# The down projection of a gated FFN as one stage of seven block products by tokens, on one Trainium2 core

## The chip, the cores and the metric

The kernel runs on one core of a Trainium2 chip. The metric is the device time of one execution in microseconds (us). A core has TensorE (PE; its weight loads are shown apart as PEld), VectorE (DVE), ScalarE (ACT), GpSimd (POOL) and SyncE (SP, which here only issues DMAs); each works through its own list of instructions in order and waits on semaphores.

## The reference

One encoder block on 512 tokens of width 1024, in float32. Three token mixers are merged and projected; then comes the part that matters here, a feed-forward layer of width 2816, and a final norm:

```python
def conv_glu_ffn(h, w_up, w_conv, b_conv, w_down):
    a, u = jnp.split(h @ w_up, 2, axis=-1)
    return (jax.nn.gelu(dwconv3(a, w_conv, b_conv)) * u) @ w_down

x = x + merged @ w_out[l]
x = x + conv_glu_ffn(rms_norm(x, ffn_norm_g[l]), w_ffn_up[l], w_ffn_conv[l], b_ffn_conv[l], w_ffn_down[l])
return rms_norm(x, final_norm_g)
```

## The kernel before, in words

Activations lie with features on the 128 partitions and the 512 tokens along the free dimension: a tile is 128 features x 512 tokens. Every float32 product is made of three matmuls (`mm3`, lines 212 to 215): each operand is split into a rounded high part and the rest. For weights, ACT copies the raw tile to the high part (L195) and DVE subtracts (L196); high and low tiles have four slots each (`hi`, `lo`). For activations `split_act` does the same (L219, L220). SP loads the raw weights (L159) into three buffers, three blocks ahead. Scratch of 128x512 (`scr`, seven buffers) and large `unit` tiles (fifteen of 2112 columns) come from pools; PSUM has two pools of four banks (`mmps`, `atps`).

`x2` holds the residual stream after the mixers, features by tokens, eight tiles. The FFN runs in two halves of eleven feature tiles (`for hh in range(2)`). For each feature tile f, two up projections (`ua`, `uu`: 24 matmuls each) are followed by a chain: DVE scales and convolves (`conv`: L458, ACT L460, L461, L462), ACT and DVE make the gelu (L1414 to L1417), POOL multiplies by the norm factor `rb2` (L1418), DVE multiplies by the second projection (L1421), and the result U is split (L219, L220). After each half comes its down projection: eight output tiles of 11 x 3 matmuls, added to `x2` by DVE (L1428). In the second half the last tiles are handled by `last_tiles`: tiles 5, 6 and 7 for the first 256 tokens, tile 5 for the rest, then, for the last two blocks of 128 tokens, the last two tiles by tokens, with the norm's sums, the scaling and the stores in between. The squares for the final norm are summed over features (`acc3`); the stores go to three outputs, two of them by features, that the host puts together.

A scheduler places the instructions: it sets the order on each engine before the run, from the program's dependences and its own estimates; the source's order is a priority, not a promise.

Of the kernel before, what the change touches and what calls it, by code (L numbers as in the profile page):

```python
# [11 lines left out]
F32 = mybir.dt.float32  # L12
# [14 lines left out]
LF = KT - 2  # L27
# [35 lines left out]
def block_list():  # L63
# [39 lines left out]
BCOLS = {n: (lambda k: P) for n in ("mlk", "o", "xaq", "memk", "naq", "nak", "g", "out", "ua", "uu", "dn")}  # L103
# [3 lines left out]
BCOLS["dnl"] = lambda k: 256  # L107
# [3 lines left out]
def hybrid_block(ctx, tc, xg, xT, memT, wflat, vecs, gbias, nabias, outa, outb, outc):  # L111
# [55 lines left out]
    lw = []  # L167

    def lastw(k, m):

        if not lw:
            lw.extend(unit(F32R) for _ in range(4))
        q = slice(k % 8 * 256, k % 8 * 256 + m)
        return lw[k // 8][:, HI256:][:, q], lw[2 + k // 8][:, q]

    def emit_split(i):
# [47 lines left out]
    gbf = cp.tile([P, 272], F32, name="gbf")  # L224
    gb, gfin = gbf[:, :16], gbf[:, 16:]
# [224 lines left out]
    SY.dma_start(gbf, gbias.partition_broadcast(P))  # L450
# [803 lines left out]
    acc3 = cp.tile([P, S], F32, name="acc_3", tag="acc", bufs=1)  # L1254
    x2v = [u[:, :4 * S].rearrange("p (f s) -> p f s", f=4) for u in x2u]

    Hf = S // 2
    half = {}

    def power(v):  # L1260
        col = tiny(v.shape[-1])
        G.tensor_tensor(col, v, nhalf[:, :v.shape[-1]], op=ALU.pow)
        return col

    def last_tiles(U, UL_):

        ws = [w for i in range(3) for w in weights(("dnl", i))]
        w5 = weights(("dn", 1, LF - 1, 0)) + weights(("dn", 1, LF - 1, 1))  # L1270

        def half_tile(f, cs, at={}):
            ps = mmps()[:, :Hf]
            fs = slice((f - LF) * P, (f - LF + 1) * P) if f >= LF else slice(0, P)
            for k in range(HF):
                w = ws[k] if f >= LF else w5[k]
                mm3(ps, w[0][:, fs], w[1][:, fs], U[k][:, cs], UL_[k][:, cs], k == 0, k == HF - 1)
                if k in at:
                    at[k]()
            xf = x2[f][:, cs]  # L1280
            V.tensor_tensor(xf, ps, xf, op=ALU.add)
            sq = scr(Hf)
            A.activation(sq, xf, AF.Square)
            V.scalar_tensor_tensor(acc3[:, cs], acc3[:, cs], EPS * D / P if f == KT - 1 else 0.0, sq, op0=ALU.add, op1=ALU.add)
            A.activation(xf, xf, AF.Copy, scale=vcol("fin_g", f))

        for f in range(LF - 1, KT):
            half_tile(f, slice(0, Hf))

        parts = two_parts(acc3[:, :Hf], Hf)  # L1290

        def sum_a(i):
            if i == 0:
                half["s"] = atps()
            PE.matmul(half["s"][:, :Hf], onesr, parts[i], start=i == 0, stop=i == 1)
            if i == 1:
                half["r"] = rstd_wide(half["s"], Hf, None)

        def scale_a(eng, *tiles):
            for i in tiles:  # L1300
                eng.tensor_tensor(x2[i][:, :Hf], x2[i][:, :Hf], half["r"], op=ALU.mult)

        def store_a(i):
            SY.dma_start(outa[i * P:(i + 4) * P, :].rearrange("(f p) s -> p f s", p=P), x2v[i // 4][:, :, :Hf])

        half_tile(LF - 1, slice(Hf, S), {5: lambda: sum_a(0), 7: lambda: sum_a(1)})
        def out_a(i):
            scale_a(V, *range(i, i + 4))
            store_a(i)

        out_a(0)
        def row_b():

            pb = atps()
            PE.matmul(pb[:, :P], ones, half["e"], start=True, stop=True)
            o, tsl = half["o"], slice(2 * P, 3 * P)
            for u, n in ((0, 4), (1, LF - 4)):
                V.tensor_tensor(o[:, u * S:u * S + n * P].rearrange("p (f s) -> p f s", f=n), x2v[u][:, :n, tsl],
                                pb[:, :P].unsqueeze(1).to_broadcast([P, n, P]), op=ALU.mult)
            SY.dma_start(outc[:, :LF * P], o[:, :LF * P])  # L1320

        banks = [mmps(), mmps()]
        for t in range(2, NT):
            tsl = slice(t * P, (t + 1) * P)
            last = t == NT - 1
            bank = banks[t - 2]
            ps = bank[:, :256]
            pts = [atps() if last else None, mmps()]
            r = scr(256)

            def turn(i):
                PE.transpose(pts[i // 4][:, i % 4 * P:(i % 4 + 1) * P], x2[i][:, tsl], ident)

            def sums(sl):
                pc = atps()
                PE.matmul(pc[:, :1], acc3[:, sl], ones[:, 0:1], start=True, stop=True)
                v0 = tiny(1)
                V.tensor_scalar(v0, pc[:, :1], 1.0 / D, EPS, op0=ALU.mult, op1=ALU.add)
                return v0

            for k in range(HF):
                mm3(ps, U[k][:, tsl], UL_[k][:, tsl], ws[k][0], ws[k][1], k == 0, k == HF - 1)
                if k == 1 and last:

                    for i in range(LF, KT):
                        PE.matmul(ps[:, (i - LF) * P:(i - LF + 1) * P], x2[i][:, tsl], ident, start=False, stop=False)
                elif k == 1:
                    for i in range(LF, KT):
                        turn(i)
                    A.activation(r, pts[1][:, 256:], AF.Copy)  # L1350
                if not last and k == 4:
                    v0 = sums(tsl)

                    v1 = sums(slice(S - P, S))
                    V.scalar_tensor_tensor(banks[1][:, 256:257], v1, D ** 0.5, power(v1), op0=ALU.mult, op1=ALU.mult)
                    out_a(4)
                if last and k == 7:
                    row_b()
            if last:
                for i in range(LF):  # L1360
                    turn(i)
            sq, v = scr(257), tiny(1)
            if last:
                oa, ob = scr(), scr()

                A.activation(sq, bank[:, :257], AF.Square, scale=D ** -0.5, accum_out=v)
                A.activation(oa[:, 256:], pts[0][:, 256:], AF.Copy)
                col = power(v)
                A.activation(oa[:, :256], pts[0][:, :256], AF.Copy, scale=col)
                first = V.tensor_scalar(oa[:, 256:], oa[:, 256:], col, None, op0=ALU.mult).ins  # L1370
                SY.dma_start(outb[:, :512], oa)

                with tc.issue_after(first):
                    V.scalar_tensor_tensor(ob[:, 256:], ps, col, gfin, op0=ALU.mult, op1=ALU.mult)
                A.activation(ob[:, :256], pts[1][:, :256], AF.Copy, scale=col)
                A.dma_start(outb[:, 512:], ob)
                continue
            V.tensor_tensor(r, ps, r, op=ALU.add)
            ss = tiny(1)
            A.activation(sq[:, :256], r, AF.Square, accum_out=ss)  # L1380
            V.tensor_scalar(v, ss, 1.0 / D, v0, op0=ALU.mult, op1=ALU.add)
            col = power(v)
            half["e"] = scr(P)
            V.tensor_scalar(half["e"], ident, col, None, op0=ALU.mult)
            half["o"] = o = unit()
            V.scalar_tensor_tensor(o[:, LF * P:D], r, col, gfin, op0=ALU.mult, op1=ALU.mult)
            SY.dma_start(outc[:, LF * P:], o[:, LF * P:D])

    for hh in range(2):
        gu = [unit(F32R) for _ in range(6)]  # L1390
        UH = [gu[k // 4][:, (k % 4) * S:(k % 4 + 1) * S] for k in range(HF)]
# [162 lines left out]
```

## Time and profile before

| | |
|---|---|
| time, median of 3 runs | 873.49 us (873.18 to 873.82) |
| profiled execution, span from first to last instruction | 871.2 us; the rest of its time is not on the page, the median lies 2.3 us above the span |
| busy | PE 865.8, PEld 733.9, DVE 594.7, ACT 467.8, POOL 125.4 us |
| granted TensorE clock | 1.000 |
| DMA | 99.81 MB, mean 115 GB/s |

Rows of the profile: a group's row has line, engine, operation, what it writes and reads with shapes, count, busy time, mean duration in ns, then the idle time of the engine just before these instructions and what ended most of it. A row of the timeline has start, duration, engine, line and operation, and in brackets the wait before it. Matmul rows overlap: their pitch is the distance of starts.

### The profile page before, as it was taken

Reading aid. Unit: us, or ns where it says so; the run is one execution under the profiler, and the core shown is the slowest. Engines: PE = TensorE matmul, PEld = TensorE weight load, DVE = VectorE, ACT = ScalarE, POOL = GpSimd, SP = SyncE. Lnnn points to the kernel's source line nnn. Section 1 sums busy time; section 2 is a strip of 40 time slices with the busy share of each in tenths; the row PEclk is TensorE's granted clock in tenths of the full one; section 3 lists DMA queues with packets and bytes.
Section 4 is the critical chain, followed back from the end, with each engine's and each line's share of the span. In section 5 each row is a group of like instructions: output and inputs, shape, how many; then the busy total and the mean of one; then the engine's idle time right before and its main releaser. Section 6 shows DMA issues by size and latency. Waiting matters only on the chain.

```text
span 871.2 us, 12230 instructions
## 1 busy us (share of the span) xinstructions
PE 865.8 (99%) x4287; PEld 733.9 (84%) x4287; DVE 594.7 (68%) x1292; ACT 467.8 (54%) x981; POOL 125.4 (14%) x202
## 2 busy tenths in 40 slices
PE   9999999999999999999999999999999999999997
PEld 7898889888888888888888888888888888888887
DVE  7794698997477768897676558776633466666534
ACT  7563577764355658897534455444422344444532
POOL 0101100000344370600000002111100011111010
PEclk9999999999999999999999999999999999999999
DMA  8324643533343453533223433323233323232412
GB/s 281 101 75 147 196 140 89 169 107 115 93 132 82 113 146 112 160 116 122 99 96 109 144 109 97 98 96 98 78 98 113 102 96 97 96 98 87 141 35 97
DMA packets 39421, 99.81 MB, mean 115 GB/s; under 512 B 5688, under 2 KB 13880, under 8 KB 39360
## 3 DMA queue, kind: packets, MB, share of 16 engines
q1 hardware_dynamic: 31568, 92.32, 32.6%
q0 software_dynamic: 7360, 6.32, 3.4%
q8 instruction: 34, 0.56, 0.3%
q10 hardware_dynamic: 432, 0.39, 0.1%
q14 instruction: 27, 0.22, 0.1%
HBM read 94.80 MB, written 4.21 MB: 114 GB/s over the span
## 4 chain that ended last, share of the span: by engine, by line
PE 98%; DVE 1%; issue 0%; ACT 0%; POOL 0%; POOLq 0%
PE mm L213 29%; PE mm L215 29%; PE mm L214 29%; PE at L214 2%; PE at L213 2%; PE at L215 2%; PE at L982 1%; PE at L963 1%; PE at L944 0%; PE at L945 0%; PE at L765 0%; PE at L813 0%; PE at L1070 0%; PE at L243 0%; PE mm L422 0%
## 5 line engine op out<-in xcount | busy, mean ns | idle before, releaser
L213 PE MATMUL mm<-u,wh 128*128 128x512 f32 (+1 forms) x1072 | 414.3, 386 | 0.0
L215 PE MATMUL mm<-u,wl 128*128 128x512 f32 (+1 forms) x1072 | 411.8, 384 | 0.0
L214 PE MATMUL mm<-u,wh 128*128 128x512 f32 (+1 forms) x1072 | 411.5, 384 | 0.0
L195 ACT ACTIVATE wh<-wr 128x512 fp32r<-128x512 f32 (+2 forms) x298 | 184.2, 621 | 219.9 <-PE mm L214 177.2
L196 DVE TENSOR_TENSOR wl<-wr,wh 128x512 fp32r<-128x512 f32 (+3 forms) x300 | 203.4, 681 | 88.5 <-ACT wh L195 86.4
L215 PEld LDWEIGHTS mm<-u,wl 128*128 128x128 f32 x1072 | 201.3, 188 | 40.3 <-DVE wl L196 0.4
L213 PEld LDWEIGHTS mm<-u,wh 128*128 128x128 f32 x1072 | 201.5, 188 | 39.0 <-ACT wh L195 0.4
L214 PEld LDWEIGHTS mm<-u,wh 128*128 128x128 f32 x1072 | 201.5, 188 | 38.5
L1418 POOL TENSOR_TENSOR s<-s,rb 128x512 f32<-128x512 f32 x22 | 38.2, 1736 | 401.7 <-DVE s L1417 238.9
L540 POOL DMA_DIRECT2D u<-nav_d x128 | 62.5, 535 | 70.5 <-DVE X L220 24.3
L219 ACT ACTIVATE u<-s 128x512 fp32r<-128x512 f32 x26 | 16.4, 632 | 56.4 <-DVE s L1421 56.3
L1421 DVE TENSOR_TENSOR s<-mm,s 128x512 f32<-128x512 f32 x22 | 15.2, 690 | 23.9 <-POOL s L1418 23.9
L460 ACT ACTIVATE s<-pad,vec 128x512 f32<-128x512 f32 x30 | 24.4, 813 | 9.7 <-DVE pad L458 9.7
L220 DVE SCALAR_TENSOR_TENSOR u<-s,u 128x512 fp32r<-128x512 f32 x26 | 19.1, 733 | 14.8 <-ACT u L219 14.5
L461 DVE SCALAR_TENSOR_TENSOR s<-pad,vec,s 128x512 f32<-128x512 f32 x30 | 22.5, 750 | 5.5 <-ACT s L460 5.5
L1417 DVE SCALAR_TENSOR_TENSOR s<-s,s 128x512 f32<-128x512 f32 x22 | 15.2, 691 | 13.4 <-ACT s L1416 13.3
L462 DVE SCALAR_TENSOR_TENSOR s<-pad,vec,s 128x512 f32<-128x512 f32 x30 | 22.5, 750 | 0.9
L1416 ACT ACTIVATE s<-s 128x512 f32<-128x512 f32 x22 | 13.9, 632 | 14.9 <-DVE s L1415 14.9
L1196 DVE TENSOR_TENSOR s<-mm,rb_x 128x512 f32<-128x512 f32 x16 | 11.0, 689 | 13.8 <-PE mm L215 13.7
L458 DVE TENSOR_TENSOR pad<-mm,rb 128x512 f32<-128x512 f32 x22 | 15.1, 690 | 6.4 <-PE mm L215 6.2
L1428 DVE TENSOR_TENSOR u<-mm,u 128x512 f32<-128x512 f32 x13 | 9.0, 692 | 14.6 <-PE mm L215 14.6
L214 PE MATMUL mm<-wl,u 128*128 128x512 f32 x48 | 18.7, 390 | 0.0
(352 smaller groups left out, 1053.3 us busy)
## 6 DMA issues: line engine op xcount, KB each, us to landing
wr<-wflat SPq DMA_DIRECT2D x141, 512.0 KB, 3.3
nab<-nabias SPq DMA_DIRECT2D x16, 256.0 KB, 2.7
u<-nav_d POOLq DMA_DIRECT2D x128, 32.0 KB, 2.8
s<-xT SPq DMA_DIRECT2D x15, 256.0 KB, 4.0
wr<-wflat SPq DMA_DIRECT2D x14, 192.0 KB, 2.4
nav_d<-nv POOLq DMA_DIRECT2D x8, 256.0 KB, 2.5
R<-rd SPq DMA_DIRECT2D x8, 256.0 KB, 4.6
wr<-wflat SPq DMA_DIRECT2D x2, 544.0 KB, 3.4
```

What stands on the lines that cost most here:

```text
L195: A.activation(h[:, u:v], src, AF.Copy)
L196: V.tensor_tensor(l[:, u:v], src, h[:, u:v].bitcast(F32), op=ALU.subtract)
L213: PE.matmul(ps, lh, rh, start=start, stop=False)
L214: PE.matmul(ps, lh, rl, start=False, stop=False)
L215: st["mm"] = PE.matmul(ps, ll, rh, start=False, stop=stop).ins
L219: A.activation(h, src, AF.Copy, scale=scale)
L220: V.scalar_tensor_tensor(l, src, scale, h.bitcast(F32), op0=ALU.mult, op1=ALU.subtract)
L460: A.activation(t1, pad[:, 0:512], AF.Identity, scale=vcol(w, i), bias=vcol(b, i))
L461: V.scalar_tensor_tensor(t1, pad[:, 1:513], vcol(w, n + i), t1, op0=ALU.mult, op1=ALU.add)
L462: V.scalar_tensor_tensor(t1, pad[:, 2:514], vcol(w, 2 * n + i), t1, op0=ALU.mult, op1=ALU.add)
L540: G.dma_start(vw[r * 32:(r + 1) * 32, i * 256:(i + 1) * 256], nav_v[hf, r, CW[b]:CW[b] + 32, hp * 256:(hp + 1) * 256])
L1418: G.tensor_tensor(c, c, rb2, op=ALU.mult)
```

## The change

The two halves are put one behind the other: all 22 up tiles first, U kept unsplit (`UR`), then one down stage. That stage multiplies U (512 tokens x 2816) by the down weights (2816 x 1024) as 2 x 2 blocks of 256 tokens x 1408 and 1408 x 512. Seven products of sums and differences of blocks (p1, p5, p6, p3, p7, p2, p4) take the place of eight. Now the stationary operand is U and the output lies by tokens: for each product eleven weight tiles of 128x512, each feeding two blocks of 128 tokens, six matmuls. Before this:

- `turn` transposes `x2` into `xt` (tokens on partitions) on PE, 32 transposes of 128x128 in eight groups between up tiles, each with an ACT copy.
- `sum_load` reads the four weight blocks (1 MB per step, eleven steps), POOL makes four subtractions of 128x512 for each, and a DMA from POOL's queue writes the sums to the DRAM tile `tdn` (1 MB per step). The down stage reads its weights, 512 columns wide, from `wdn` or `tdn`.
- `ops_to` makes the U operand of a product: some are U's blocks, some are sums made by POOL (p5 and p3 in scratch, p6 in place of a11) or by DVE (a21 for p7, in place), then split by ACT and DVE.
- `tiles_to` splits the weight tiles: ACT copies, DVE subtracts, or POOL for each fourth tile in p1, p7, p2 and p4.
- `add` puts the products together: DVE adds from PSUM into `xt` or the partial sum Q (kept in scratch), POOL adds Q into `xt`.

The final norm is by tokens: ACT squares with a sum along the row, POOL's power, scaling by ACT or DVE, and four stores by rows (the last one in two parts). The host no longer turns anything.

```diff
+        def store():
+            G.tensor_tensor(q[B21], q[B21], q[B22], op=ALU.subtract)
+            G.dma_start(tdn[:, :, k * S:(k + 1) * S].rearrange("q p n -> p q n"), w.rearrange("p (q n) -> p q n", q=4))
+        sums.extend([lambda: G.tensor_tensor(q[B11], q[B12], q[B11], op=ALU.subtract),
+                     lambda: G.tensor_tensor(q[B12], q[B22], q[B12], op=ALU.subtract),
+                     lambda: G.tensor_tensor(q[B22], q[B22], q[B11], op=ALU.subtract), store])
...
+PRODUCTS = (("p1", wdn, B11), ("p5", tdn, T1), ("p6", tdn, T2), ("p3", wdn, B22), ("p7", tdn, T3), ("p2", wdn, B21),
+            ("p4", tdn, T4))
...
+            A.activation(h, src, AF.Copy)
+            eng = G if k % 4 == 3 and PRODUCTS[p][0] in ("p1", "p7", "p2", "p4") else V
+            eng.tensor_tensor(l, src, h.bitcast(F32), op=ALU.subtract)
...
+            if name == "p6":
+                G.tensor_tensor(a11, a22, a21, op=ALU.subtract)
...
+                    if name == "p5":
+                        G.tensor_tensor(t, a21[:, sl], a22[:, sl], op=ALU.add)
+                    else:
+                        G.tensor_tensor(t, a12[:, sl], a11[:, sl], op=ALU.subtract)
...
+            if name == "p5":
+                V.tensor_tensor(a21, a11, a21, op=ALU.subtract)
...
-            V.tensor_tensor(c, pu, c, op=ALU.mult)
-            split_act(UH[j], UL[j], c, 0.5)
-        for f in range(KT if hh == 0 else LF - 1):
-            ws = weights(("dn", hh, f, 0)) + weights(("dn", hh, f, 1))
-            ps = mmps()
-            for k in range(HF):
-                mm3(ps, ws[k][0], ws[k][1], UH[k], UL[k], k == 0, k == HF - 1)
-            V.tensor_tensor(x2[f], ps, x2[f], op=ALU.add)
...
+        for _ in range(3):
+            if sums:
+                sums.pop(0)()
...
+        V.scalar_tensor_tensor(UR[f], pu, 0.5, c, op0=ALU.mult, op1=ALU.mult)
+        if 2 <= f < 10:
+            turn(f - 2)
...
+            if name in ("p6", "p7"):
+                V.tensor_tensor(Q[t], ps, Q[t], op=ALU.add)
+            for c in {"p1": ((0, 0),), "p5": ((0, 1), (1, 1)), "p3": ((0, 1),), "p2": ((0, 0),)}.get(name, ()):
+                V.tensor_tensor(cell(c, t), ps, cell(c, t), op=ALU.add)
+            for c in {"p6": ((0, 1),), "p7": ((1, 1), (1, 0))}.get(name, ()):
+                G.tensor_tensor(cell(c, t), cell(c, t), Q[t], op=ALU.add)
...
+        if k == 7 and name == "p2":
+            for t in (2, 3):
+                squares(t, part[t], S, D)
+                V.tensor_tensor(xt[t][:, S:], xt[t][:, S:], gfin[:, S:], op=ALU.mult)
```

Three places in the engines' lists. First, DVE from the last up tile into the down stage. Before (wl: a weight's low part, pad and s: the chain of one up tile, the first u: U's low part):

```order
L196 TENSOR_TENSOR wl_7584<-wr_7493,wh_7583 128x512
L1421 TENSOR_TENSOR s_7529<-mm_7549,s_7529 128x512
L220 SCALAR_TENSOR_TENSOR u_6903<-s_7529,u_6900 128x512
L196 TENSOR_TENSOR wl_7626<-wr_7539,wh_7625 128x512
L458 TENSOR_TENSOR pad_140<-mm_7587,rb_5628 128x512
L196 TENSOR_TENSOR wl_7630<-wr_7539,wh_7629 128x512
```

Now, from the gelu of the last up tile (u_5547 and u_5911 hold a21, u_7507 is p1's operand, u_7417 and u_7419 raw weights of p1):

```order
L1356 SCALAR_TENSOR_TENSOR s_7459<-s_7459,s_7455 128x512
L1326 TENSOR_TENSOR u_5547<-u_5547 128x4x256
L1358 SCALAR_TENSOR_TENSOR s_7455<-s_7459,s_7455 128x512
L1326 TENSOR_TENSOR u_5911<-u_5911 128x4x256
L1367 SCALAR_TENSOR_TENSOR u_7254<-mm_7473,s_7455 128x512
L1324 TENSOR_TENSOR u_7507<-u_5911,u_7507 128x1024
L1293 TENSOR_TENSOR wl_7525<-u_7419,wh_7524 128x512
L1293 TENSOR_TENSOR wl_7535<-u_7419,wh_7534 128x512
L1293 TENSOR_TENSOR wl_7545<-u_7419,wh_7544 128x512
L1324 TENSOR_TENSOR u_7556<-u_6285,u_7556 128x768
```

Two in-place differences and the operands' low parts now stand between the weights' low parts. Second, POOL at the same place. Before, only the products with `rb2`, one per up tile, and then sums of squares:

```order
L1418 TENSOR_TENSOR s_7613<-s_7613,rb_5628 128x512
L1418 TENSOR_TENSOR s_7697<-s_7697,rb_5628 128x512
L1418 TENSOR_TENSOR s_7781<-s_7781,rb_5628 128x512
L1436 TENSOR_TENSOR acc_5544<-acc_5544,s_7934 128x512
L1436 TENSOR_TENSOR acc_5544<-acc_5544,s_7989 128x512
```

Now, from the third of p5's sums (L1317); the last product with `rb2` (L1359) stands behind the rewriting of a11 (L1309), and p3's sums (L1319) follow:

```order
L1317 TENSOR_TENSOR s_7612<-u_5911,u_6910 128x512
L1317 TENSOR_TENSOR s_7614<-u_5911,u_6910 128x512
L1317 TENSOR_TENSOR s_7656<-u_6285,u_7254 128x512
L1309 TENSOR_TENSOR u_5547<-u_6560,u_5547 128x4x256
L1359 TENSOR_TENSOR s_7455<-s_7455,rb_5625 128x512
L1293 TENSOR_TENSOR wl_7515<-u_7417,wh_7514 128x512
L1317 TENSOR_TENSOR s_7658<-u_6285,u_7254 128x256
L1309 TENSOR_TENSOR u_5911<-u_6910,u_5911 128x4x256
L1293 TENSOR_TENSOR wl_7570<-u_7419,wh_7569 128x512
L1309 TENSOR_TENSOR u_6285<-u_7254,u_6285 128x3x256
L1319 TENSOR_TENSOR s_7848<-u_6560,u_5547 128x512
L1319 TENSOR_TENSOR s_7850<-u_6560,u_5547 128x512
```

POOL's list is now a run of whole-tile operations, with two of p1's weight subtractions in it. Third, ACT in p2, which has no counterpart before (wh: weights' high parts, u_8258, u_8311 and u_8346: p4's operand, u_5545: the last two token tiles):

```order
L1322 ACTIVATE u_8311<-u_6910 128x1024
L1291 ACTIVATE wh_8220<-u_8123 128x512
L1399 ACTIVATE s_8296,y_8295<-u_5545 128x512
L1399 ACTIVATE s_8300,y_8299<-u_5545 128x512
L1291 ACTIVATE wh_8230<-u_8123 128x512
L1322 ACTIVATE u_8346<-u_7254 128x768
```

The squares of two token tiles stand between the copies of p2's fifth and sixth weight tile.

More of the change, by code (lines that the diff above doesn't have):

```diff
@@ L1251, in hybrid_block @@
             V.scalar_tensor_tensor(acc2, acc2, EPS * D / P if f == 1 else 0.0, sq, op0=ALU.add, op1=ALU.add)
[L1254 to L1262, printed above, removed]
-        return col
[L1265 to L1274, printed above, removed]
-            for k in range(HF):
[L1276 to L1387, printed above, removed]
@@ new lines, in hybrid_block, with turn @@
+    xtu = [unit(), unit()]
+    xt = [xtu[t // 2][:, t % 2 * D:(t % 2 + 1) * D] for t in range(NT)]
+    def turn(i):
+        t, hf = divmod(i, 2)
+        pt = atps()
+        for j in range(4):
+            PE.transpose(pt[:, j * P:(j + 1) * P], x2[4 * hf + j][:, t * P:(t + 1) * P], ident)
+        A.activation(xt[t][:, hf * S:(hf + 1) * S], pt, AF.Copy)
+    HS = S // 2
+    GROUPS = ((0, 4), (4, 8), (8, HF))
+    B11, B12, B22, B21 = range(4)
+    tdn = dp.tile([4, P, HF * S], F32, name="tdn")
@@ new lines, in hybrid_block, with cell, add @@
+    gfin = wp.tile([P, BW], F32, tag="raw", name=nm("wr"), bufs=3)[:, :D]
+    SY.dma_start(gfin, gbias[16:].partition_broadcast(P))
+    banks, Q = {}, []
+    def cell(c, t):
+        return xt[2 * c[0] + t][:, c[1] * S:(c[1] + 1) * S]
+    def add(name):
+        for t in range(2):
+            ps = banks[name][t]
+            if name == "p1":
+                Q.append(scr())
+                A.activation(Q[t], ps, AF.Copy)
+            if name in ("p6", "p7"):
[4 more added lines that the diff above has]
+                G.tensor_tensor(cell(c, t), cell(c, t), Q[t], op=ALU.add)
@@ new lines, in squares, with power, finish @@
+    def squares(t, n, c0, c1):
+        s = tiny(1)
+        A.activation(scr(c1 - c0), xt[t][:, c0:c1], AF.Square, scale=D ** -0.5, accum_out=s)
+        n.append(s)
+    def power(n):
+        v, col = tiny(1), tiny(1)
+        V.tensor_scalar(v, n[0], n[1], EPS, op0=ALU.add, op1=ALU.add)
+        for s in n[2:]:
+            V.tensor_tensor(v, v, s, op=ALU.add)
+        G.tensor_tensor(col, v, nhalf[:, :1], op=ALU.pow)
+        return col
+    def finish(t):
+        n = []
+        squares(t, n, 0, S)
+        squares(t, n, S, D)
+        col = power(n)
+        V.scalar_tensor_tensor(xt[t], xt[t], col, gfin, op0=ALU.mult, op1=ALU.mult)
+        SY.dma_start(out[t * P:(t + 1) * P, :], xt[t])
@@ new lines, in hybrid_block, with mms @@
+    part = {2: [], 3: []}
+    TAIL = HF - 4
+    def mms(p, k, t, cs=slice(0, S), ps=None, first=0, end=HF - 1):
+        name = PRODUCTS[p][0]
+        g, kk = divmod(k, 4)
+        h, l = ops[p, g]
+        wh, wl = wsp[p, k]
+        q = slice(kk * HS + t * P, kk * HS + (t + 1) * P)
+        mm3(banks[name][t] if ps is None else ps, h[:, q], l[:, q], wh[:, cs], wl[:, cs], k == first, k == end)
+    for j, (p, k) in enumerate(TILES):
+        name = PRODUCTS[p][0]
+        last = name == "p4"
+        if k == 0:
+            pool = atps if name in ("p1", "p5", "p7", "p2") else mmps
+            banks[name] = [pool(), pool()]
+        if k % 4 == 0:
+            i = STEPS.index((p, k // 4))
+            raws_to(i + 4)
+            ops_to(i + 2 if i == 0 else i + 3)
+        tiles_to(j + 4)
+        if k == 3 and p > 0:
+            add(PRODUCTS[p - 1][0])
+        if k == 7 and name == "p2":
+            for t in (2, 3):
+                squares(t, part[t], S, D)
+                V.tensor_tensor(xt[t][:, S:], xt[t][:, S:], gfin[:, S:], op=ALU.mult)
+        if k == 7 and last:
+            for t in range(2):
+                finish(t)
+        if last and k >= TAIL:
+            if k == HF - 1:
+                V.tensor_tensor(cell((1, 0), 1), banks["p4"][1], cell((1, 0), 1), op=ALU.add)
+                for kk in range(TAIL, HF):
+                    mms(p, kk, 0)
+                ends = [mmps(), mmps()]
+                for e in range(2):
+                    for kk in range(TAIL, HF):
+                        mms(p, kk, 1, slice(e * HS, (e + 1) * HS), ends[e][:, :HS], TAIL)
+            continue
+        mms(p, k, 0)
+        mms(p, k, 1, end=TAIL - 1 if last else HF - 1)
@@ new lines, in hybrid_block @@
+    for t in (2, 3):
+        x, n = xt[t], part[t]
+        for ps, c in ((banks["p4"][0], (0, S)),) if t == 2 else zip((e[:, :HS] for e in ends), ((0, HS), (HS, S))):
+            V.tensor_tensor(x[:, slice(*c)], ps, x[:, slice(*c)], op=ALU.add)
+            squares(t, n, *c)
+        if t == 3:
+            v, col = tiny(1), tiny(1)
+            V.tensor_scalar(v, n[0], n[1], EPS, op0=ALU.add, op1=ALU.add)
+            V.tensor_tensor(v, v, n[2], op=ALU.add)
+            G.tensor_tensor(col, v, nhalf[:, :1], op=ALU.pow)
+        else:
+            col = power(n)
+        A.activation(x[:, S:], x[:, S:], AF.Copy, scale=col)
+        V.scalar_tensor_tensor(x[:, :S], x[:, :S], col, gfin[:, :S], op0=ALU.mult, op1=ALU.mult)
+        if t == 2:
+            SY.dma_start(out[t * P:(t + 1) * P, :], x)
+        else:
+            SY.dma_start(out[t * P:(t + 1) * P, :S], x[:, :S])
+            A.dma_start(out[t * P:(t + 1) * P, S:], x[:, S:])
```

196 lines of the change are left out of this document (109 added, 87 removed).

## The prediction

> **What bounds the kernel now.** I read the spans first, then the busy times, the chain that ended last, and a table by stage (505 to 614 first half of the up projections, 614 to 676 its down products, 676 to 803 the second half, then its down products and the end; columns: busy time and instructions of PE, PEld, DVE, ACT, POOL, granted clock, DMA share, GB/s).
>
> ```profile
> core 0: 871.2 us, clock 1.000
> PE 865.8 (99%) x4287; PEld 733.9 (84%) x4287; DVE 594.7 (68%) x1292; ACT 467.8 (54%) x981; POOL 125.4 (14%) x202
> PE 98%; DVE 1%; issue 0%; ACT 0%; POOL 0%; POOLq 0%
> 505.00:614.00 109.00, 109.00 (x482) 90.28 (x481) 79.40 (x117) 54.81 (x87) 15.46 (x10) 1.00 0.29 94
> 614.00:676.00 62.00, 62.00 (x275) 51.33 (x274) 25.25 (x40) 17.56 (x30) 2.99 (x2) 1.00 0.32 99
> 803.00:866.00 63.00, 63.00 (x382) 56.49 (x381) 28.48 (x58) 25.63 (x48) 8.23 (x7) 1.00 0.27 87
> ```
>
> TensorE is the bound from end to end, at the full granted clock: in the down stages it has no gap, while DVE is busy for 25 of 62 us and POOL for 3. So a matmul removed is time gained, as long as the other engines keep feeding it. That is the question here.
>
> **TensorE's own sum.** Matmul starts give the pitch (the busy time of a row overlaps the next).
>
> ```profile
> 803.07 0.39 PE L213 MATMUL mm<-u,wh 128*128 128x512 f32 x1
> 811.91 0.39 PE L213 MATMUL mm<-u,wh 128*128 128x512 f32 x1
> 864.88 0.28 PE L215 MATMUL mm<-u,u 128*128 128x256 f32 x1
> 865.59 0.28 PE L215 MATMUL mm<-u,u 128*128 128x256 f32 x1
> 865.71 0.60 PE L1332 MATMUL at<-ident,u 128*128 128x128 f32 x4
> 332.47 0.44 PE at L963 x4
> ```
>
> 803.07 is the first down matmul of the second half; 39 matmuls lie between it and 811.91, so 0.2267 us each at 512 columns; six between the next two, 0.118 at 256. The second half's down stage ends at 865.71: 62.6 us. The first half's is 8 x 11 x 3 = 264 matmuls x 0.2267 = 59.9. Together 122.5. The seven products are 7 x 11 x 2 x 3 = 462 matmuls, the last 12 of them cut into 24 of 256 columns: 450 x 0.2267 + 24 x 0.118 = 104.8. That saves 17.7. The eight turns of x2 add 32 transposes, 0.44 per four by the chain's row: +3.5.
>
> The end: now the last column's matmul ends its slot at 865.71 and its store is issued at 867.91, 2.2 us later.
>
> ```profile
> 865.91 0.39 ACT L1366 ACTIVATE s<-mm 128x257 f32<-128x257 f32 x1 [3.30 <-PE mm L215]
> 866.19 0.19 ACT L1366 ACTIVATION_READ_ACCUMULATOR s<-mm 128x1 f32 x1
> 866.46 0.55 POOL L1262 TENSOR_TENSOR y<-y,nhalf 128x1 f32<-128x1 f32 x1 [2.96 <-ACT s L1366]
> 867.91 0.35 ACTq L1376 DMA_DIRECT2D outb<-s  x1
> 858.22 1.42 DVE L1301 TENSOR_TENSOR u<-u,s 128x256 f32<-128x256 f32 x4
> L1416 ACT ACTIVATE s<-s 128x512 f32<-128x512 f32 x22 | 13.9, 632 | 14.9 <-DVE s L1415 14.9
> ```
>
> The new end adds x to the product first (128x256, 0.36 by L1301) and a second tiny sum (about 0.1), keeps square and power, and scales in one 0.63 copy where two followed: about 2.7, so +0.5 (0 to +1). The output DMA is the same 256 KB from the same queue: nothing. Without a stall the change gives -17.7 + 3.5 + 0.5 = -13.7 us.
>
> **What feeds TensorE.** Weight tiles have four slots, and ACT's copy waits for the slot:
>
> ```profile
> L195 ACT ACTIVATE wh<-wr 128x512 fp32r<-128x512 f32 (+2 forms) x298 | 184.2, 621 | 219.9 <-PE mm L214 177.2
> 601.82 0.63 ACT L195 ACTIVATE wh<-wr 128x512 fp32r<-128x512 f32 x1
> 602.49 0.69 DVE L196 TENSOR_TENSOR wl<-wr,wh 128x512 fp32r<-128x512 f32 x1
> ```
>
> Up to now a tile feeds 12 matmuls (2.72 us), so a freed slot is due again after 3 x 2.72 = 8.2 us, and copy and subtraction take 1.36 (601.82 to 603.18): 6.8 us of slack. In the new stage a tile feeds six matmuls (1.36 us): due after 4.1, slack 2.7. Behind that stands a cost which the old stage hardly had: DVE and POOL in each other's way.
>
> ```profile
> 528.49 0.69 DVE L1415 SCALAR_TENSOR_TENSOR s<-s,s 128x512 f32<-128x512 f32 x1
> 528.53 1.80 POOL L1418 TENSOR_TENSOR s<-s,rb 128x512 f32<-128x512 f32 x1 [162.82 <-PE mm L215]
> 529.09 1.79 DVE L196 TENSOR_TENSOR wl<-wr,wh 128x512 fp32r<-128x512 f32 x1
> 532.22 1.62 POOL L1418 TENSOR_TENSOR s<-s,rb 128x512 f32<-128x512 f32 x1 [1.88 <-DVE s L1417]
> 532.61 1.77 DVE L220 SCALAR_TENSOR_TENSOR u<-s,u 128x512 fp32r<-128x512 f32 x1
> 541.62 1.29 POOL L1418 TENSOR_TENSOR s<-s,rb 128x512 f32<-128x512 f32 x1 [7.79 <-DVE s L1417]
> 535.50 0.67 DVE L196 TENSOR_TENSOR wl<-wr,wh 128x512 fp32r<-128x512 f32 x1
> 536.10 0.68 DVE L220 SCALAR_TENSOR_TENSOR u<-s,u 128x512 fp32r<-128x512 f32 x1
> ```
>
> Alone, POOL's product takes 1.29. Started during a DVE operation on two SBUF inputs it takes 1.80: it waits for that one. The next such DVE operation then takes 1.79 instead of 0.69: it stood for 1.10. The two run in turns. Undisturbed, DVE starts one every 0.60 (535.50 to 536.10). So a shared resource is occupied 0.60 by each DVE operation of 128x512 on two SBUF inputs and 1.10 by each of POOL's; other widths in proportion (DVE 1.13 for 1024 elements, 0.87 for 768, 0.33 for 256; POOL 2.2, 1.65, 0.55: estimates from these rows).
>
> **First stall: p1 to p5.** Take time 0 where p1's first matmul could start. From L1358 of the last up tile to the subtraction of p5's fourth tile, number 14, DVE's list holds 16 such operations of 512, two of 1024, two of 768, one of 256: 9.6 + 2.3 + 1.7 + 0.3 = 13.9 us. POOL's list over the same stretch (the rewriting of a11 for p6, the last product with rb2, two weight subtractions, the rest of p5's sums, p3's sums) is eight of 512, two of 1024, one each of 768 and 256: 8.8 + 4.4 + 1.7 + 0.6 = 15.4. In turns that is 29.3, ready at about 29.5; tile 14 is due at 14 x 1.36 = 19.0. TensorE loses 10.5. Before that, POOL runs five of p5's sums while DVE is in the last up tile's chain: 5 x 1.10, of which DVE's idle time (109 - 79.4 us over ten up tiles, 3.0 each) and the dropped split of U (0.6) take 3.6: it arrives 2 us late. I take +12.5. From below: if POOL always fell into DVE's gaps, DVE's 13.9 and two PSUM additions (1.2) fit in 19.0, and nothing is lost. From above: the full 5.5 late and some idle turns, +16. I take the value nearest to 529.09 and 532.61, because POOL's list has no gaps here.
>
> The Trainium skill (SBUF — State Buffer, section "SBUF: two separate sides") describes an exclusive lock on a port pair that DVE and GpSimd share: whichever starts first holds it for its whole instruction. By that rule POOL would hold it for 1.29, its 15.4 would be 18.1, and the forecast 878.5. The trace agrees on the turns and shows 1.10 of the 1.29.
>
> **Second stall: p2.** Once p7 is done, POOL makes four additions of Q behind a weight subtraction; ACT's square of the fourth token tile waits for the third of them, and p2's sixth tile's copy stands behind that square on ACT. From p2's start: DVE's two additions to Q 1.25, POOL's subtraction to 1.75, then three additions of 1.10 in turns with DVE's next operations (1.13, 0.60, 0.60): 7.4; square 0.8, copy 0.6, subtraction 0.6: 9.4. The sixth tile is due at 6.8. +3 (0 to +4). In p6, p3 and p7 DVE needs eleven subtractions, the three of the operand (1.13, 1.13, 0.87) and up to four additions, 12.1 of 15.0 us per product, POOL 2.4, ACT about 10: nothing. In p4 the norm of two token tiles adds four squares on ACT (0.8) and two products of 1024 on DVE: they fit too.
>
> **Up stage.** It gains 44 subtractions on POOL and 11 stores, and loses the split of U. Per up tile (48 matmuls, 10.9 us) DVE holds the resource for eight operations, 4.9, POOL for three subtractions and the product with rb2, 4 x 1.10 = 4.4: it fits on average. At worst POOL has eight subtractions and two stores between two products with rb2, about 15 us with the waits, so DVE (blocked at L1367, weight subtractions behind it) gets 4 us late; the slack is 6.8. +0.5 (0 to +6). A store's issue costs POOL:
>
> ```profile
> L540 POOL DMA_DIRECT2D u<-nav_d x128 | 62.5, 535 | 70.5 <-DVE X L220 24.3 <-PE at L982 22.2 <-PE mm L215 16.6
> L530 POOL DMA_DIRECT2D nav_d<-nv x8 | 4.5, 565 | 53.5 <-DVE nv L528 52.6 <-ACT wh L195 0.9
> SPq L159 <- DVE wl L196: 291.4, 66, 7.1
> 0.00:20.00 20.00, 19.23 (x85) 14.93 (x86) 13.79 (x28) 14.77 (x26) 1.97 (x17) 1.00 0.84 285
> ```
>
> 32 KB and 256 KB cost 0.54 and 0.57, so 1 MB at least that and at most 4 x 0.57; I take 0.8. The 1 MB loads stand on SP between weight loads; at the 285 GB/s of the first 20 us one takes 3.7 us, and a weight load waits 291.4 / 66 = 4.4 us for its buffer anyway: nothing, or up to 3.7 where that cover is gone. The down stage reads 77 x 256 KB in 104.8 us, 193 GB/s, loads four steps ahead: below 285, nothing.
>
> **Sum.** -13.7 + 12.5 + 3 + 0.5 = +2.3 us: a profiled span of 873.5 after 871.2. The runs' median, 873.49, is 2.3 above that span; I keep the distance: **875.8 us**.
>
> **Rivals.**
> - *A, POOL fits into the gaps, faster.* After the first two pairs in the trace (L1418 at 550 and later) POOL waits for DVE, and no DVE operation is stretched again; DVE's own demand is under TensorE's. If POOL mostly waits, the stalls are 3 to 4 us in all: -13.7 + 3.5 = -10, 863.3 (860 to 869). Against it: that was one POOL operation per 10.9 us, now a dozen stand in a row, ready. 0.30.
> - *B, the up stage starves too, slower.* The place is the product with rb2 behind eight subtractions. It decides where DVE falls back by more than 6.8 us; four bursts that overshoot by 2 give +8: 884. The mean demand, 9.3 of 10.9, speaks against it. 0.13.
> - *C, transfers come late, slower.* Where sums, stores and weights overlap in the up stage 3.1 MB in 10.9 us are asked for, some 290 GB/s, as much as the first 20 us moved; ten late loads of 1 us give +10: 886. Against it: loads run two blocks ahead. 0.07.
>
> Forecast: 0.50, its own range 871 to 880 (stalls 11 to 20). What a measurement can tell from no change is 0.2%, 1.75 us. Of the forecast's half, 0.02 lies under 871.7 and 0.18 within 875.2; so faster 0.30 + 0.02 = 0.32, same 0.18, slower 0.30 + 0.13 + 0.07 = 0.50. Leaving out A's lowest third and half of B and C, the range is 863 to 884.
>
> **What would show it.** Right: TensorE shows its first gaps in p1 and p5's first tiles, together 10 to 15 us, released by weight subtractions of DVE or POOL; L1293 and L1324 on DVE take up to 1.8 us there; a gap of some 3 us near p2's sixth tile; no gap in the up stage. The prediction is wrong if DVE's rows stay at 0.7 beside a busy POOL (A), if matmuls wait in the up stage on L176 (B), or if ACT's copies wait for DMA (C).

## The result and the profile after

The changed kernel takes 884.26 us (882.36 to 885.15, four runs) against 873.34 in the same session: ratio 1.0123, interval 1.0109 to 1.0138. It is slower by 10.9 us, just beyond the range's upper end. The profiled execution's span went from 871.2 to 882.0 us.

The spans, the busy times, and the table by stage (505 to 751 up projections, 751 to 780 p1 and p5, 780 to 836 p6, p3 and p7 with p2's start, 836 to 856 the rest of p2 and p4's start; columns as before):

```profile
core 0: 882.0 us, clock 0.996
PE 858.5 (97%) x4146; PEld 718.5 (81%) x4146; DVE 674.0 (76%) x1306; ACT 486.6 (55%) x1015; POOL 241.6 (27%) x283
505.00:751.00 246.00, 243.11 (x1085) 200.28 (x1084) 189.80 (x226) 103.64 (x168) 117.45 (x81) 1.00 0.55 192
751.00:780.00 29.00, 21.23 (x77) 14.65 (x76) 27.05 (x24) 14.36 (x25) 19.65 (x10) 0.94 0.40 150
780.00:836.00 56.00, 54.79 (x240) 44.34 (x239) 48.71 (x67) 34.52 (x54) 9.81 (x7) 1.00 0.60 207
836.00:856.00 20.00, 16.09 (x69) 12.47 (x68) 15.16 (x17) 10.39 (x19) 9.54 (x6) 1.00 0.26 93
```

TensorE did fewer matmuls but now stands still in three places: in the up stage, in p1 and p5 (DVE busy for 27.05 of 29 us, POOL for 19.65), and in p2. What it waited for (total, times, longest):

```profile
PE at L194 <- DVE wl L1293: 5.7, 7, 1.5
PE at L194 <- POOL wl L1293: 4.2, 1, 4.2
PE mm L195 <- DVE wl L176: 2.9, 3, 2.4
PE at L193 <- ACT wh L1291: 2.5, 2, 2.2
```

A wait is not the whole loss, since some matmuls after it start more slowly. Below, "lost" is the distance between matmul starts beyond 0.2267 us (0.118 at 256 columns), summed over a stretch: 3.7 us in the up stage, 13.3 in p1 and p5 (9.6 and 3.7), 0.7 in p3, 4.8 in p2.

In p1, DVE, POOL and TensorE in the timeline:

```profile
753.67 2.76 POOL L1309 TENSOR_TENSOR u<-u,u 128x1024 f32<-128x1024 f32 x1 [3.16 <-DVE u L1326]
754.11 3.40 DVE L1326 TENSOR_TENSOR u<-u 128x1024 f32<-128x1024 f32 x1
756.39 2.24 POOL L1359 TENSOR_TENSOR s<-s,rb 128x512 f32<-128x512 f32 x1
758.60 1.26 POOL L1293 TENSOR_TENSOR wl<-u,wh 128x512 fp32r<-128x512 f32 x1
759.91 0.79 PE L194 MATMUL at<-wl,u 128*128 128x512 f32 x1 [4.19 <-POOL wl L1293]
```

DVE's L1326, which takes about 1.2 alone (1.22 at 752.38), stood for POOL's L1309; POOL's L1359 then stood for DVE; and p1's fourth low part, behind it on POOL, was ready only at 759.86.

The up stage shows something else. Here are POOL's and DVE's rows around TensorE's longest gap there (L1258 and L1261 to L1263 are the four subtractions of a sum, L1259 its store, L1359 the product with `rb2`, L176 the low part of an up weight):

```profile
622.86 0.79 POOL L1259 DMA_DIRECT2D tdn<-u  x1 [0.30 <-POOL u L1258]
623.67 1.29 POOL L1261 TENSOR_TENSOR u<-u 128x512 f32<-128x512 f32 x1
624.92 1.28 POOL L1359 TENSOR_TENSOR s<-s,rb 128x512 f32<-128x512 f32 x1
626.15 1.25 POOL L1262 TENSOR_TENSOR u<-u 128x512 f32<-128x512 f32 x1
623.03 4.93 DVE L176 TENSOR_TENSOR wl<-wr,wh 128x512 fp32r<-128x512 f32 x1
628.02 0.50 PE L195 MATMUL mm<-u,wl 128*128 128x512 f32 x1 [2.36 <-DVE wl L176]
```

One low part of 0.69 took 4.93 us: it began while POOL issued a store and came through only after three POOL operations, none of which gave it a turn. DVE was behind already from standing for the sums before, in turns:

```profile
616.18 1.82 DVE L441 SCALAR_TENSOR_TENSOR s<-pad,vec,s 128x512 f32<-128x512 f32 x1
617.93 1.78 DVE L176 TENSOR_TENSOR wl<-wr,wh 128x512 fp32r<-128x512 f32 x1
619.63 1.78 DVE L1356 SCALAR_TENSOR_TENSOR s<-s,s 128x512 f32<-128x512 f32 x1
622.11 1.00 DVE L1358 SCALAR_TENSOR_TENSOR s<-s,s 128x512 f32<-128x512 f32 x1 [0.70 <-ACT s L1357]
```

Undisturbed these take 0.75 (L441) and 0.69: 3.6 us more, and with the 4.24 behind them 7.8, which is over the slack of 6.8.

### The profile page after: what moved, and what is told of

The parts are those of the page before. It is cut to its first block, busy times and chain, and to the rows that moved or that the text cites. A ratio compares the mean times of both kernels' runs of the same rounds, so it can differ in the third digit from the quotient of the medians.

```text
span 882.0 us, 12121 instructions
## 1 busy us (share of the span) xinstructions
PE 858.5 (97%) x4146; PEld 718.5 (81%) x4146; DVE 674.0 (76%) x1306; ACT 486.6 (55%) x1015; POOL 241.6 (27%) x283
## 5 line engine op out<-in xcount | busy, mean ns | idle before, releaser
L195 PE MATMUL mm<-u,wl 128*128 128x512 f32 (+1 forms) x907 | 350.5, 387 | 2.9 <-DVE wl L176 2.9
L193 PE MATMUL mm<-u,wh 128*128 128x512 f32 (+1 forms) x907 | 353.2, 390 | 0.0
L194 PE MATMUL mm<-u,wh 128*128 128x512 f32 (+1 forms) x907 | 349.7, 386 | 0.0
L175 ACT ACTIVATE wh<-wr 128x512 fp32r<-128x512 f32 (+1 forms) x256 | 157.9, 625 | 149.9 <-PE mm L194 117.3
L176 DVE TENSOR_TENSOR wl<-wr,wh 128x512 fp32r<-128x512 f32 (+2 forms) x258 | 196.7, 765 | 47.4 <-ACT wh L175 46.2
L194 PEld LDWEIGHTS mm<-u,wh 128*128 128x128 f32 x907 | 170.6, 188 | 32.9
L193 PEld LDWEIGHTS mm<-u,wh 128*128 128x128 f32 x907 | 170.6, 188 | 32.6
L1359 POOL TENSOR_TENSOR s<-s,rb 128x512 f32<-128x512 f32 x22 | 36.3, 1648 | 250.3 <-PE mm L195 163.5
L1293 DVE TENSOR_TENSOR wl<-u,wh 128x512 fp32r<-128x512 f32 x69 | 58.6, 881 | 7.5 <-ACT wh L1291 7.3
L194 PE MATMUL at<-wl,u 128*128 128x512 f32 (+2 forms) x152 | 54.5, 359 | 10.1 <-DVE wl L1293 5.7
L1291 ACT ACTIVATE wh<-u 128x512 fp32r<-128x512 f32 x77 | 46.8, 625 | 30.5 <-PE at L195 12.9
L193 PE MATMUL at<-wh,u 128*128 128x512 f32 (+2 forms) x152 | 53.2, 350 | 2.5 <-ACT wh L1291 2.5
L195 PE MATMUL at<-wh,u 128*128 128x512 f32 (+2 forms) x152 | 52.9, 348 | 0.0
L195 PE MATMUL mm<-wh,u 128*128 128x512 f32 (+1 forms) x118 | 45.1, 382 | 0.0
L193 PE MATMUL mm<-wh,u 128*128 128x512 f32 (+1 forms) x118 | 44.9, 382 | 0.0
L1367 DVE SCALAR_TENSOR_TENSOR u<-mm,s 128x512 f32<-128x512 f32 x22 | 15.2, 691 | 26.7 <-POOL s L1359 26.7
```

Source lines behind the costliest of these rows:

```text
L175: A.activation(h[:, u:v], src, AF.Copy)
L176: V.tensor_tensor(l[:, u:v], src, h[:, u:v].bitcast(F32), op=ALU.subtract)
L193: PE.matmul(ps, lh, rh, start=start, stop=False)
L194: PE.matmul(ps, lh, rl, start=False, stop=False)
L195: st["mm"] = PE.matmul(ps, ll, rh, start=False, stop=stop).ins
L1291: A.activation(h, src, AF.Copy)
```

## The experiments

| | time, us | ratio to before | lost: up stage | p1 and p5 | p2 |
|---|---|---|---|---|---|
| changed kernel | 884.26 | 1.0123 | 3.7 | 13.3 | 4.8 |
| e1 low parts on DVE | 880.75 | 1.0087 (1.0072 to 1.0102) | 3.5 | 12.4 | 2.2 |
| e2 operand sums on DVE | 874.59 | 1.0015 (1.0003 to 1.0026) | 3.3 | 3.5 | 4.8 |
| e3 squares later | 883.14 | 1.0114 (1.0097 to 1.0131) | 4.6 | 13.3 | 3.8 |
| e4 no weight sums | 880.42 | 1.0085 (1.0070 to 1.0100) | 0 | 13.3 | 4.8 |
| e5 all of it on DVE | 862.98 | 0.9883 (0.9866 to 0.9899) | 0 | 1.2 | 0 |
| e6 down stage's part on DVE | 866.60 | 0.9924 (0.9909 to 0.9939) | 3.3 | 1.2 | 0 |
| e7 weight sums on DVE | 880.44 | 1.0085 (1.0070 to 1.0100) | 0 | 13.3 | 6.8 |
| e8 no stores | 880.03, one run | | 0 | 13.3 | 4.8 |
| e9 no operand sums | 868.20, one run | | 3.8 | 0.4 | 2.1 |
| e10 unread sums on POOL | 879.38, one run | | 6.3 | 8.7 | 2.1 |
| e11 e6, stores from SP | 863.32 | 0.9884 (0.9868 to 0.9900) | 0 | 1.3 | 0 |

**e1.**

```diff
-            eng = G if k % 4 == 3 and PRODUCTS[p][0] in ("p1", "p7", "p2", "p4") else V
+            eng = V
```

> All low parts of the down weights are made by DVE (eight subtractions leave POOL, two of them in p1). Theory 'turns' (DVE operations on two SBUF inputs and POOL operations occupy one resource, 0.60 and 1.10 us each, so the first tiles are late by the sum of both lists): p1's 4.2 us wait for POOL's low part goes, but the sum of both lists falls only by 2 x 0.5 us, so p1 and p5 still lose 11 to 12 us instead of 13.0; time 882 to 883. Rival 'POOL's list' (TensorE waits only because the low part of p1's fourth tile stands behind the rewriting of a11 and the last product with rb2 on POOL): the 4.2 us are gained whole, p1 and p5 lose 8 to 9 us; time 879 to 880.

The time came between the two. The place decides: p1 and p5 kept 12.4 of 13.3 us; the wait only changed its name.

```profile
PE at L194 <- DVE wl L1293: 9.8, 6, 5.7
PE mm L195 <- DVE wl L176: 2.6, 2, 2.2
```

So the wait for POOL's low part alone does not explain p1. The gain lay in p2 (4.8 to 2.2), which neither theory had named.

**e2.**

```diff
-                G.tensor_tensor(a11, a22, a21, op=ALU.subtract)
+                V.tensor_tensor(a11, a22, a21, op=ALU.subtract)
...
-                        G.tensor_tensor(t, a21[:, sl], a22[:, sl], op=ALU.add)
+                        V.tensor_tensor(t, a21[:, sl], a22[:, sl], op=ALU.add)
...
-                        G.tensor_tensor(t, a12[:, sl], a11[:, sl], op=ALU.subtract)
+                        V.tensor_tensor(t, a12[:, sl], a11[:, sl], op=ALU.subtract)
```

> The operand sums of p5, p6 and p3 (L1317, L1309, L1319) are made by DVE instead of POOL. Theory 'turns': twelve microseconds of POOL become 6.6 of DVE; the sum of both lists up to p5's fourth tile falls from 29.3 to about 25 against 19.0 due, so p1 and p5 lose about 6 us instead of 13.0; time about 877. Rival 'DVE is the bound there' (POOL's operations run beside DVE's at little cost and DVE's own list is what is late): DVE gets 6.6 us more in the same stretch, the loss grows to 15 us or more; time 886 or more.

DVE, the busier engine, got more work, and p1 and p5 lose 3.5 us instead of 13.3, less than the 6 expected. DVE as the bound by itself falls.

**e3.**

```diff
-        if k == 7 and name == "p2":
+        if k == 1 and last:
```

> The squares of the last two token tiles and their products with gfin are moved from p2's eighth tile to p4's second. Theory 'ACT's square blocks the copy' (the square waits for POOL's addition of Q, p2's sixth tile's copy stands behind it): p2's 4.7 us go, up to 1 us comes back in p4; time about 880. Rival 'the additions themselves' (four Q additions on POOL in turns with DVE's low parts make p2 late without any square): the low parts of p2's tiles stay late, 3 us or more of the 4.7 stay; time 883.

The rival holds: 3.8 of 4.8 us stay. Without the square, p2's low parts are late beside POOL's additions of Q, in POOL's and DVE's timeline of e3:

```profile
842.67 7.61 POOL L1395 TENSOR_TENSOR u<-u,s 128x512 f32<-128x512 f32 x4
843.72 1.77 DVE L1293 TENSOR_TENSOR wl<-u,wh 128x512 fp32r<-128x512 f32 x1
845.41 2.04 DVE L1324 TENSOR_TENSOR u<-u,u 128x768 fp32r<-128x768 f32 x1
847.38 1.75 DVE L1293 TENSOR_TENSOR wl<-u,wh 128x512 fp32r<-128x512 f32 x1
```

**e4.**

```diff
-            G.tensor_tensor(q[B21], q[B21], q[B22], op=ALU.subtract)
...
-        sums.extend([lambda: G.tensor_tensor(q[B11], q[B12], q[B11], op=ALU.subtract),
-                     lambda: G.tensor_tensor(q[B12], q[B22], q[B12], op=ALU.subtract),
-                     lambda: G.tensor_tensor(q[B22], q[B22], q[B11], op=ALU.subtract), store])
+        sums.append(store)
```

> Leaves out the sums of the down weights in the up stage (44 POOL subtractions); the 1 MB loads and the stores stay, so the products use unsummed blocks. Theory 'turns': the three gaps of the up stage (2.5, 0.5 and 0.3 us, with their slower restarts 3.7 us) go and no DVE row of 128x512 there lies above 1.8 us; time about 880.5. Rival 'traffic' (the loads and stores of the sums delay DVE's list or the weights): the gaps stay; time 884.

The gaps went, traffic and all stores present: POOL's work is needed for them. Whether as turns or with the store's issue, e8 tells.

**e5, e6, e7.** e6 is e1 and e2 together with

```diff
-                G.tensor_tensor(cell(c, t), cell(c, t), Q[t], op=ALU.add)
+                V.tensor_tensor(cell(c, t), cell(c, t), Q[t], op=ALU.add)
```

e7 has V for G in the four subtractions of `sum_load` alone; e5 is both.

> All two-operand work that the change gave to POOL goes to DVE: the sums of the down weights, the operand sums, the eight low parts, the additions of Q. POOL keeps the product with rb2 and the stores. Theory 'turns': an operation costs 0.60 instead of 1.10 and nobody stands in turn, so the up stage's 3.7 us go, p1 and p5 lose 2 to 3 us instead of 13.3, p2 0 to 1 instead of 4.8; time about 866, faster than the kernel before the change. Rival 'DVE becomes the bound': 44 sums more in the up stage come in bursts and 5 us or more are lost there and in p6 to p7, where DVE had no idle time left; time 871 or more.

> Only the down stage's POOL work goes to DVE (operand sums, low parts, additions of Q); the sums of the down weights stay on POOL in the up stage. Theory 'turns': the gains of the down stage alone, 10.5 in p1 and p5 and 4 in p2; the up stage keeps its 3 to 4 us; time about 869.5. Rival 'DVE becomes the bound': p6 to p4 lose 3 us or more; time 873.

> Only the sums of the down weights go from POOL to DVE. Theory 'turns': DVE has 3.0 us idle in each up tile and the sums take 4 x 0.60 in two of three tiles, so the up stage loses under 1 us instead of 3.7; time about 880.5. Rival 'DVE becomes the bound': the bursts of up to eight subtractions (4.8 us) in front of low parts cost 4 us or more; time 884 or more.

All three went as 'turns' said, e5 and e6 by 3 us further. e7's profile is of the longest of its four executions, 882.10 us: p2 lost 2 us more there than in the changed kernel, at a granted clock of 0.50 from 846.6 to 853.4. e5 is the fastest kernel, 1.2% (10.3 us) under the kernel before the change. Its busy times, the low parts of the down weights, and all that TensorE waits for (L222 is the program's start):

```profile
PE 852.4 (99%) x4146; PEld 718.3 (83%) x4146; DVE 661.2 (77%) x1379; ACT 492.4 (57%) x1015; POOL 127.2 (15%) x210
L1293 DVE TENSOR_TENSOR wl<-u,wh 128x512 fp32r<-128x512 f32 x77 | 50.5, 684 | 3.2 <-ACT wh L1291 3.0
PE at L222 <- PEq L1578: 0.8, 1, 0.8
PE at L194 <- DVE wl L1293: 0.8, 1, 0.8
```

DVE runs 73 more operations (x1379 after x1306) and is busy for 12.8 us less. A low part takes 684 ns; in the changed kernel it was

```profile
L1293 DVE TENSOR_TENSOR wl<-u,wh 128x512 fp32r<-128x512 f32 x69 | 58.6, 881 | 7.5 <-ACT wh L1291 7.3
```

**e8.**

```diff
-            G.dma_start(tdn[:, :, k * S:(k + 1) * S].rearrange("q p n -> p q n"), w.rearrange("p (q n) -> p q n", q=4))
...
```

(The rest of the edit has `wdn` for `tdn` in `PRODUCTS`.)

> Leaves out the eleven stores of the sums (and reads the unsummed blocks in their place); POOL's 44 subtractions in the up stage stay. In the changed kernel each DVE operation of 2.2 us or more in the up stage began 0.17 us after the start of such a store's issue on POOL (549.12 and 549.29, 622.86 and 623.03). Theory 'turns alone': the gaps come from the subtractions themselves and 2.5 us or more stay in the up stage. Rival 'the store's issue opens the way': a subtraction that stands ready behind the issue takes the resource ahead of DVE; without the issue no 128x512 row of DVE there lies above 1.9 us, and under 1 us is lost.

The rival holds: with all 44 subtractions still on POOL, the up stage loses nothing, and the wait on L176 is gone from the list (line numbers are one lower here: L1292 is the changed kernel's L1293). It takes both, the subtractions (e4) and the issue of the store (e8).

```profile
PE at L194 <- DVE wl L1292: 5.6, 7, 1.5
PE at L194 <- POOL wl L1292: 4.2, 1, 4.2
PE at L193 <- ACT wh L1290: 2.5, 2, 2.2
```

**e9, e10.** Both are e1 with the operand sums gone; e10 puts POOL work of nearly the same size in their place.

```diff
-                G.tensor_tensor(a11, a22, a21, op=ALU.subtract)
...
-                        G.tensor_tensor(t, a21[:, sl], a22[:, sl], op=ALU.add)
...
-                        G.tensor_tensor(t, a12[:, sl], a11[:, sl], op=ALU.subtract)
+            if name == "p6" or srcs[0][2] is None:
+                y = a22 if name in ("p5", "p6") else a12
+                for k in range(0, nk, 2):
+                    m = min(2, nk - k)
+                    G.tensor_tensor(r3(spare[:, :m * HS]), y[:, k:k + m], y[:, k:k + m], op=ALU.add)
...
```

(The added lines are e10's alone; in both runs p5, p6 and p3 then take a block of U as it is.)

> As e1 (all low parts on DVE), and the operand sums of p5, p6 and p3 are left out: the products take unsummed blocks, and POOL has nothing in p1 to p3. It is the floor for e10. Both theories: p1 and p5 lose 1 to 2 us instead of e1's 12.3; time about 869.

> As e9, but POOL does as many additions of the same size as the operand sums, into a spare tile that nobody reads (p6's as 512 columns each). Twelve of them stand behind the last product with rb2, 11 x 1.10 us. Nothing waits for their results. Theory 'turns': DVE's operations still stand for them; DVE's 16.3 us and POOL's 12.7 up to p5's fourth tile are 29 against 19.0 due, p1 and p5 lose 8 us or more; time about 877. Rival 'POOL's results come late' (TensorE lost its time because DVE and ACT waited for sums that POOL makes slowly): p1 and p5 lose 1 to 2 us as in e9; time about 869.

Work whose result nobody reads costs 8.3 us in p1 and p5 (8.7 less 0.4). DVE's timeline in e9 (three low parts of weights at L1293, two of operands at L1314), then POOL's and DVE's in e10 (the same at L1294 and L1320), where the same pieces of work take 4.42 instead of 1.88 and 2.54 instead of 1.28:

```profile
754.77 1.88 DVE L1293 TENSOR_TENSOR wl<-u,wh 128x512 fp32r<-128x512 f32 x3
758.04 1.28 DVE L1314 TENSOR_TENSOR u<-u,u 128x512 fp32r<-128x512 f32 x2
```

```profile
757.92 18.29 POOL L1313 TENSOR_TENSOR spare<-u 128x256 f32<-128x256 f32 x13 [1.76 <-DVE u L1363]
769.88 4.42 DVE L1294 TENSOR_TENSOR wl<-u,wh 128x512 fp32r<-128x512 f32 x3
774.22 2.54 DVE L1320 TENSOR_TENSOR u<-u,u 128x512 fp32r<-128x512 f32 x2
```

So 8.3 of the 12.0 us by which e1 loses more than e9 are DVE standing for POOL. The other 3.7 are not separated: in e10 nobody waits for the sums, but five of them also run earlier there, in the up stage (from 662.07 on), where e1 has its five directly before p1 (742.44). That late results make the 3.7 is not shown. The 6.3 us of e10's up stage were not followed further.

**e11.**

```diff
-            G.dma_start(tdn[:, :, k * S:(k + 1) * S].rearrange("q p n -> p q n"), w.rearrange("p (q n) -> p q n", q=4))
+            SY.dma_start(tdn[:, :, k * S:(k + 1) * S].rearrange("q p n -> p q n"), w.rearrange("p (q n) -> p q n", q=4))
```

(on e6)

> e6 (the down stage's POOL work on DVE, the sums of the down weights still on POOL) with the stores of the sums issued on SP's queue instead of POOL's. Theory 'the store's issue opens the way' (e8): the up stage loses nothing, no DVE row of 128x512 above 1.9 us there; time 863.2. Rival 'SP's queue': a store waits there for POOL's sums, and the weight loads behind it come late, 2 us or more; time 865 or more.

As expected: the sums may stay on POOL if the store is issued elsewhere. 863.32 and e5's 862.98 differ by 0.04%, too little to tell apart here.

## Why the prediction was wrong

| term, us of the profiled span | forecast | measured |
|---|---|---|
| seven products without stalls | -17.7 | -17.7 |
| transposes in the up stage, other delays before p1 | +3.5 | +4.4 |
| p1 and p5 | +12.5 | +13.3 |
| p3 | 0 | +0.7 |
| p2 | +3 | +4.8 |
| up stage | +0.5 | +3.7 |
| the end | +0.5 | +1.7 |
| sum | +2.3 | +10.9 |

The products: from p1's first matmul at 751.26 to the end of the last one's slot at 874.87 (it starts at 874.75 and has 0.118) are 123.6 us; less 18.8 lost there, 104.8 stand, as forecast. The +4.4 is the later start of p1 (751.26 after 803.07 - 59.9 = 743.2) less the up stage's 3.7. The transposes themselves make 3.8 of it: in e8, whose up stage loses nothing else, the 1056 up matmuls and 32 transposes before p1 take 243.2 us, and 1056 x 0.2267 is 239.4. Another 0.3 was lost in the first 24 us of the execution, far ahead of the changed stages.

**Right:** the bound, the matmul count, the first stall in place, mechanism and size, and that no transfer held TensorE up. The row 3.40 of L1326, and e2 and e10, confirm that DVE and POOL take turns. By the whole-instruction reading of the Trainium skill (SBUF — State Buffer, "SBUF: two separate sides") the stall would have been 15.2; 13.3 lies nearer to the 12.5 from the rows, though waits for results may be in it too. Rival A falls: POOL did not fit into gaps that were not there.

**The step that failed: "Up stage ... +0.5".** It measured +3.7. Its own range, 0 to +6, held that, but the sum took nearly nothing and the sign "no gap in the up stage" was wrong. The step let DVE wait at most one POOL operation at a time and looked for trouble only on average and at the product with `rb2`. DVE was held for up to three operations in a row behind a store's issue (4.93 us instead of 0.69), and it was late already when that began. No row of before showed it: there POOL issued only transfers of 8 to 256 KB, all of them before the up stage. I priced the issue at 0.8 us of POOL's time (it takes 0.79). Rival B gave 884 us, close to the result, and its signs came: matmuls waited in the up stage on L176, and DVE fell back by more than 6.8 us. But its mechanism was another, eight subtractions in front of the product with `rb2`. e8 keeps those and loses nothing, so B's cause fell. Its number is a coincidence too: B put all of the extra 8 us into the up stage, which lost 3.7.

That step is 3.2 of the 8.6 us by which the sum was short. Five smaller misses, all the same way, are the rest: p2 1.8, the end 1.2, the delays before p1 0.9, p1 and p5 0.8, and p3 0.7, which the forecast put at nothing (e2 has 0.1 there; the cause was not followed). TensorE's stalls came to 22.5 us, where the forecast had 16.0 and its own range 11 to 20.

**Mis-sized:** p2, where I put the loss down to ACT's square alone. That wait came (2.2 us at ACT's copy), but e3 shows another directly behind it: DVE's low parts in turns with four additions of Q. Then the end, whose rows are:

```profile
874.84 0.75 DVE L1475 SCALAR_TENSOR_TENSOR u<-u,y,wr 128x512 f32<-128x512 f32 x1 [0.66 <-POOL y L1407]
875.51 0.42 DVE L1465 TENSOR_TENSOR u<-mm,u 128x256 f32<-128x256 f32 x1
877.33 0.75 DVE L1475 SCALAR_TENSOR_TENSOR u<-u,y,wr 128x512 f32<-128x512 f32 x1 [0.67 <-POOL y L1471]
878.11 0.33 SPq L1479 DMA_DIRECT2D out<-u  x1
```

The addition to the last product stands behind the scaling of the third token tile on DVE (875.51, the last matmul's slot ends at 874.87), and the store is issued 3.2 us after that slot instead of the 2.7 worked out. The other 0.7 comes behind the issue, 0.5 of it the output's landing (2.8 us now, 2.3 before, for 256 KB each), which I had taken as unchanged. No run tried this end alone.

With -17.7 + 4.4 + 1.7 the change is worth 11.6 us of the span, and e5, which loses 1.8 in the down stage, gets 10.2 of them (861.0 after 871.2). The idea was sound; what cost its gain was the engine chosen for the elementwise work.

## What to carry to other kernels

Price an operation moved to POOL by what it takes from DVE, here up to 1.10 us for each 128x512, against 0.60 if DVE does it itself: if DVE feeds the bound, give the work to DVE even when DVE is the busier engine, as long as its list still fits (in e5 it was busy for 77% of the span). Do not issue a large store from POOL with arithmetic ready behind it while DVE is on a tight schedule; SP's queue issued it here at no cost. When a product is made cheaper in matmuls, count the feeding work per matmul first: a weight tile here fed six instead of twelve, and the slack went from 6.8 to 2.7 us.

## What was unexpected in the hardware

**A store's issue on POOL takes DVE's turn away.** In the changed kernel four DVE operations of 128x512 in the up stage took 2.5 us or 4.93; each began 0.17 us after an issue that had a POOL operation ready behind it. Other DVE operations that began beside an issue with nothing ready behind took their usual time (606.46, the convolution's L440, 0.74). So did one in e7 (663.64, 0.69), where the POOL operation behind the issue started right after it but became ready only while DVE's was running. Why the waiting DVE operation is not served first was not settled.

**The clock falls after short gaps.** After p1's 4.2 us gap the matmuls from 760.51 to 762.64 start 0.43 us apart instead of 0.23. The table by stretch of the changed kernel (granted clock third from the end), there and in p2:

```profile
759.60:762.90 3.30, 2.98 (x7) 2.41 (x8) 3.30 (x3) 2.33 (x4) 3.30 (x3) 0.50 0.00 0
846.00:853.00 7.00, 3.14 (x12) 1.72 (x10) 4.56 (x6) 4.12 (x8) 4.48 (x4) 1.00 0.00 0
```

And e2 in p2, the matmul behind the gap in its timeline and the same table:

```profile
838.39 0.64 PE L193 MATMUL at<-wh,u 128*128 128x512 f32 x1 [2.17 <-ACT wh L1291]
```

```profile
838.60:842.00 3.40, 3.32 (x7) 1.82 (x6) 3.40 (x4) 2.38 (x5) 1.42 (x1) 0.50 0.01 2
```

The same gap in the changed kernel's p2 (846 to 853) left the clock at 1.00. A drop did not always cost time: p2 lost 4.8 us in both of these executions, and 6.8 in e7, where the clock stayed at 0.50 for 6.8 us behind a gap of the same 2.2. The changed kernel's runs span 2.8 us, those of e5, without such gaps, 0.34; that the clock makes this difference is not shown, for the shortest of the changed kernel's runs (882.36) has the lowest mean clock of the four (0.989). The Trainium skill (TensorE: Matmul & The Clock Gate, "The HAM clock gate") has half clock after an idle window of about 3.4 us that runs freely. Half-clock stretches of that length are in these traces (838.6 to 842.0 above), but they followed idle times of 2.2 us too.
